# First norm of a hybrid decoder block: order of loads, two projections side by side, squares summed on GpSimd, masks moved in the program

## The chip, the cores and the metric

The kernel runs on one core of a Trainium2 chip. A core has five engines that each work through their own list of instructions in order: PE (TensorE, matmuls; PEld is its weight load), DVE (VectorE), ACT (ScalarE), POOL (GpSimd) and SP (SyncE, which here only issues DMA transfers). They wait for each other through semaphores. The metric is the device time of one execution in microseconds (us); lower is better.

## The reference

The block computes, for x of 512 tokens by 1024:

```python
h = rms_norm(x, ln1_g)                 # y = x * rsqrt(mean(x*x) + eps) * g
p = h @ w_in                           # 2464 columns
y_rwkv = rwkv7_mixer(p_rwkv, ...)      # token shift, decay, recurrence over 8 heads
y_attn = rms_norm(swa_sink_attention(q, k, v, sinks), attn_norm_g)
x = x + concatenate([y_rwkv, y_attn]) @ w_out
x = x + peer_ffn(rms_norm(x, ln2_g), ...)   # product-key choice of 128 of 16384 experts per token
return rms_norm(x, lnf_g)
```

Only the first two lines, and the constants that the mixer needs later, are touched by the change.

## The kernel before

The work runs in one line of stages: the first norm with the projections and the RWKV mixer (up to some 200 us), attention and the recurrence, the output projection with the second norm, the key products with the choice of experts, and from some 420 us to the end the experts themselves, dense matmuls over all experts for 384 tokens and gathered rows for the other 128. Each stage needs the result of the one before.

The first norm is laid out transposed: `xT` is eight tiles of 128 model columns by 512 tokens (k = 0 to 7). Per k, line 269 multiplies by ln1_g (tile `h`, DVE), `split` (lines 166 and 167) makes a high part `hhi` (a cast on ACT) and a low part `hlo` (a subtraction on DVE), and `take` squares the raw tile on ACT (lines 216 and 219) and adds the square to `n1acc` (line 220). The tiles of the squares, `n1sq`, have three buffers, so the square of k waits until the one of k - 3 has been added. The scale of the tokens, 1/rms, is applied after the projection: `scale` sums `n1acc` over the partitions with four small matmuls (`n1ss`, line 225) and takes the inverse root in twelve small DVE steps (`rsq`); `spread` brings the result to all partitions by four matmuls (`n1b`, line 232), and ACT copies it to `rb` (line 283). Every projection is multiplied by `rb` when it leaves PSUM (line 307, `pr`).

A projection (`mm3_`, lines 176 to 178) is three matmuls of 128x512 for each k: high by high, low by high, high by low. Its weights come in two halves of 256 KB, `w`, three buffers; each half is split in the same way into `wh` and `wl`, four buffers each. Projection 0 feeds the low-rank paths (`la`, then `lw` and the four `pld` products of line 330), projection 3 the first group's `k`.

On GpSimd, constants are made: identity, masks, `id32` (line 134) and the five levels of `lmask` (lines 142 to 147: for each level and quarter a memset and two affine selects), which a 32 by 32 inverse in the mixer uses from about 60 us on.

The order of instructions on each engine in this stage is not the order of the program text: a scheduler in the build sets it, engine by engine, from priorities and from its own estimates of when things are ready. Only PE's order inside the block `manual_schedule` around projection 0, `scale` and `spread` follows the text, and later projections' matmuls may still be put between. Once built, the order is fixed, and each engine takes it as it stands.

Of the kernel before, what the change touches and what calls it, by code (L numbers as in the profile page):

```python
# [7 lines left out]
F32 = mybir.dt.float32  # L8
# [9 lines left out]
S = 512  # L18
# [57 lines left out]
def _emit(ctx, tc, A, out, dbg, stop):  # L76
# [15 lines left out]
    xT = xp.tile([128, KD, S], F32, name="xT")  # L92
    vec = consts.tile([128, NVEC], F32, name="vec")
    SY.dma_start(vec, A["vec"])
    for k in range(2):
        SY.dma_start(xT[:, k, :], A["xT"][:, k, :])
    sink = consts.tile([128, 8], F32, name="sink")

    def vcol(c):
        return vec[:, c:c + 1]  # L100
# [24 lines left out]
    bones = consts.tile([128, 128], F32, name="bones")  # L125
    V.tensor_copy(bones[:, 0:64], hind[:, 0:1].to_broadcast([128, 64]))
    V.tensor_copy(bones[:, 64:128], hind[:, 1:2].to_broadcast([128, 64]))


    lmask = consts.tile([128, 5, 32], F32, name="lmask")  # L130
    id32 = consts.tile([128, 32], F32, name="id32")
    for q in range(4):
        rows = slice(32 * q, 32 * q + 32)
        GP.affine_select(out=id32[rows], in_=ones[rows, :32], pattern=[[1, 32]],
                         compare_op=OP.is_equal, fill=0.0, base=0, channel_multiplier=-1)
    for lv in range(5):
        b = 1 << lv
        n = 32 // (2 * b)
        for q in range(4):
            rows = slice(32 * q, 32 * q + 32)  # L140
            m = lmask[rows, lv, :].rearrange("p (n w) -> p n w", w=2 * b)
            GP.memset(lmask[rows, lv, :], 0.0)

            GP.affine_select(out=m[:, :, b:2 * b], in_=ones[rows, :n * b].rearrange("p (n w) -> p n w", w=b),
                             pattern=[[-2 * b, n], [0, b]], compare_op=OP.is_ge, fill=0.0,
                             base=0, channel_multiplier=1)
            GP.affine_select(out=m[:, :, b:2 * b], in_=m[:, :, b:2 * b],
                             pattern=[[2 * b, n], [0, b]], compare_op=OP.is_ge, fill=0.0,
                             base=b - 1, channel_multiplier=-1)

    c_ = consts.tile([128, 64], F32, name="c_")
    omu = c_[:, 0:14]
# [11 lines left out]
    def split(dst_hi, dst_lo, src, hi_eng=None, lo_eng=None):  # L164

        (hi_eng or SC.copy)(dst_hi, src)  # L166
        (lo_eng or V).tensor_tensor(out=dst_lo, in0=src, in1=dst_hi.bitcast(F32), op=OP.subtract)  # L167
# [40 lines left out]
    def rms(pool, n, width, name, add_eng):  # L208
# [26 lines left out]

        return take, scale, spread

    def load_w(src, name="w"):
        his, los = [], []
        for hf in range(2):  # L240
            ks = slice(4 * hf, 4 * hf + 4)
            w = wst.tile([128, 4, 128], F32, name=name, tag="w", bufs=3)
            SY.dma_start(w, src[:, ks])
            whi = wst.tile([128, 4, 128], F32R, name=name + "h", tag="wh", bufs=4)
            wlo = wst.tile([128, 4, 128], F32R, name=name + "l", tag="wl", bufs=4)
            split(whi, wlo, w)
            his += [whi[:, k] for k in range(4)]
            los += [wlo[:, k] for k in range(4)]
        return his, los

    first = {}

    def proj(i, m=128):
        whi, wlo = first.pop(i) if i in first else load_w(A["w_in"][i])
        p = pt("proj", "pj")
        yield from mm3_(p[:m], whi, wlo, hhi, hlo, m=m)
        return p[:m]


    first[0] = load_w(A["w_in"][0])  # L260
    for k in range(2, KD):
        SY.dma_start(xT[:, k, :], A["xT"][:, k, :])
    SY.dma_start(sink, A["sink"])

    take, scale, spread = rms(xp, KD, D, "n1", V)
    hhi, hlo = hl("h")
    for k in range(KD):
        h = xp.tile([128, S], F32, name="h", tag="h", bufs=3)
        V.tensor_scalar(h, xT[:, k, :], vcol(C_LN1 + k), None, op0=OP.mult)
        split(hhi[:, k, :], hlo[:, k, :], h)  # L270
        take(k, xT[:, k, :])
    with tc.manual_schedule(engines={mybir.EngineType.PE}):
        p0 = proj(0)
        while True:
            try:
                next(p0)
            except StopIteration as e:
                p0 = e.value
                break
        scale()  # L280
        pb = spread()
    rb = prep.tile([128, S], F32, name="rb", tag="rb")
    SC.copy(rb, pb)
    xst.close()

    def weave(a, na, b, nb):

        i = j = 0
        while a or b:
            if a and (not b or i * nb <= j * na):  # L290
                i += 1
                if next(a, self_) is self_:
                    a = None
            else:
                j += 1
                if next(b, self_) is self_:
                    b = None
# [22 lines left out]
    ld = [prep.tile([128, S], F32, name=f"ld{t}", tag=f"ld{t}") for t in range(NT)]  # L320

    def lora():
        yield from shifted(0, la, prep, p=p0)
        lw = prep.tile([128, S], F32, name="lw", tag="t2")
        SC.activation(lw, la, AF.Tanh)
        GP.memset(lw[64:96, :], 1.0)

        for t in range(NT):
            p = pt("chain", "pld")
            mm(p, lw[:, t * 128:(t + 1) * 128], wup, start=True, stop=True)  # L330
            SC.activation(ld[t], p, AF.Tanh, scale=0.5)
            V.tensor_scalar(ld[t], ld[t], 0.5, 0.5, op0=OP.mult, op1=OP.add)
            yield
# [11 lines left out]

    def prepare(j):
        k = prep.tile([128, S], F32, name="k", tag="k", bufs=2)
        yield from shifted(2 + 3 * j + 1, k, prep)
        kk = rwk.tile([128, S], F32, name=f"kk{j}")
        SC.activation(kk, k, AF.Identity, scale=vcol(C_KK + j))  # L350
        sq = prep.tile([128, S], F32, name="ksq", tag="t1")
        SC.activation(sq, k, AF.Square, scale=vcol(C_KK + j))
        pss = pt("chain", "kss", (128, NT, 2))
        for t in range(NT):
            mm(pss[:, t, :], sq[:, t * 128:(t + 1) * 128], hind, start=True, stop=True)
        kn = work.tile([128, NT, 2], F32, name="kn", tag="kn")
        rsqrt(kn.rearrange("p t e -> p (t e)"), pss.rearrange("p t e -> p (t e)"), 2 * NT, floor=1e-24)
        pn = pt("chain", "pn")
        for t in range(NT):
            for e in range(2):  # L360
                mm(pn[64 * e:64 * e + 64, t * 128:(t + 1) * 128], kn[:, t, e:e + 1].to_broadcast([128, 64]), ident,
                   start=True, stop=True)
        V.tensor_tensor(out=kk, in0=kk, in1=pn, op=OP.mult)
        yield
        r = prep.tile([128, S], F32, name="r", tag="r", bufs=1)
        yield from shifted(2 + 3 * j, r, prep)
        v = prep.tile([128, S], F32, name="v", tag="v", bufs=2)
        yield from shifted(2 + 3 * j + 2, v, prep)
        cs = slice(j * 128, (j + 1) * 128)

        pa = pt("chain", "pa")
        mm(pa, aup[:, cs], la, start=True, stop=True)
        B = prep.tile([128, S], F32, name="B", tag="B", bufs=2)
        SC.activation(B, pa, AF.Tanh, scale=0.5, bias=ha0[:, j:j + 1])
        kf = prep.tile([128, S], F32, name="kf", tag="t2")
        SC.activation(kf, B, AF.Identity, scale=hka[:, j:j + 1], bias=ohka[:, j:j + 1])
        V.tensor_tensor(out=k, in0=k, in1=kf, op=OP.mult)
        V.tensor_scalar(B, B, -0.5, -0.5, op0=OP.mult, op1=OP.add)
        V.tensor_tensor(out=B, in0=B, in1=kk, op=OP.mult)

        pl = pt("chain", "pl")
        for t in range(NT):
            mm(pl[:, t * 128:(t + 1) * 128], ld[t][:, cs], incl, start=True, stop=True)
        E = prep.tile([128, 8, 65], F32, name="E", tag="E", bufs=1)
        GP.memset(E[:, :, 0:1], 1.0)
        SC.activation(E[:, :, 1:65], c8(pl), AF.Exp, scale=DECAY)
        Ei = prep.tile([128, S], F32, name="Ei", tag="Ei", bufs=1)
        SC.activation(Ei, pl, AF.Exp, scale=-DECAY)
        GP.tensor_copy(DC[:, :, j:j + 1], E[:, :, 64:65])
        AR = rwk.tile([128, 8, 128], F32, name=f"AR{j}")  # L390
        V.tensor_tensor(out=AR[:, :, 0:64], in0=c8(kk), in1=E[:, :, 0:64], op=OP.mult)
        V.tensor_tensor(out=AR[:, :, 64:128], in0=c8(r), in1=E[:, :, 1:65], op=OP.mult)
        ARs.append(AR)
        V.tensor_tensor(out=B, in0=B, in1=Ei, op=OP.mult)

        V.scalar_tensor_tensor(r, r, vcol(C_RK + j), k, op0=OP.mult, op1=OP.mult)
        pbn = pt("chain", "pbn")
        mm(pbn, bones, r, start=True, stop=True)
        V.tensor_tensor(out=kk, in0=pbn, in1=v, op=OP.mult)
        BVs.append(kk)  # L400
        V.tensor_tensor(out=k, in0=k, in1=Ei, op=OP.mult)
        ops[j] = k, v, B, AR
        yield
# [1084 lines left out]
```

## Time and profile before

| | us |
|---|---|
| time, median of 3 runs | 1632.48 (1631.82 to 1632.66) |
| the profiled execution's own time | 1630.73 |
| its span, first to last instruction | 1629.0 |
| PE busy | 1572.6 (97%) |
| DVE busy | 1286.1 (79%) |
| POOL busy | 742.4 (46%) |
| ACT busy | 652.5 (40%) |

The profile is taken in one execution; all times below are counted from the start of its span. Busy time of an engine adds up its instructions; matmuls overlap, so their starts (the pitch from one to the next) say more than their lengths. A row of the timeline gives start, length, engine, line, operation, what is written and read, how many instructions are merged in it, and in brackets how long the engine sat idle before and what ended that.

### The profile page before, as it was taken

How to read it: one execution, taken by the hardware profiler on the slowest of the kernel's cores; microseconds unless marked ns; L12 is line 12 of the kernel's file. 1: busy time of each engine (PE TensorE's matmuls, PEld its weight loads, DVE VectorE, ACT ScalarE, POOL GpSimd, SP SyncE). 2: the span in 40 equal slices, each digit the busy share in tenths (PEclk: the TensorE clock that was granted, in tenths of full speed). 3: DMA queues.
4: the chain of work that ended last, by engine and by line, in shares of the span. 5: the costliest groups of instructions: out<-in, count | busy, mean ns of one | idle time of the engine just before them, and what ended most of it. 6: DMA issues, size and time to landing. Idle time of an engine off the chain costs nothing.

```text
span 1629.0 us, 30768 instructions
## 1 busy us (share of the span) xinstructions
PE 1572.6 (97%) x11869; PEld 1366.7 (84%) x11869; DVE 1286.1 (79%) x2497; ACT 652.5 (40%) x1092; POOL 742.4 (46%) x711
## 2 busy tenths in 40 slices
PE   7999999899999889999999999999999999999997
PEld 4777777797999888888988888888888888888886
DVE  6666567756899999999677788777878877887896
ACT  5333345544444344454433333333333333333334
POOL 5121123244676512222155555555655556556582
PEclk9999999999999999999999999999999999999999
DMA  4111110333232269999999888889998988989793
GB/s 143 53 42 42 59 48 2 129 124 103 79 104 91 98 214 336 348 323 354 320 345 351 304 309 320 322 299 316 331 308 301 333 312 303 321 303 339 236 311 136
DMA packets 180548, 371.18 MB, mean 228 GB/s; under 512 B 17840, under 2 KB 102320, under 8 KB 180144
## 3 DMA queue, kind: packets, MB, share of 16 engines
q1 hardware_dynamic: 137488, 226.71, 40.6%
q0 software_dynamic: 36864, 134.23, 22.9%
q10 hardware_dynamic: 6048, 8.26, 1.4%
q8 instruction: 93, 1.52, 0.4%
q14 instruction: 55, 0.45, 0.1%
HBM read 333.62 MB, written 35.52 MB: 227 GB/s over the span
## 4 chain that ended last, share of the span: by engine, by line
PE 50%; DVE 11%; DMA 3%; issue 1%; ACT 1%; POOL 1%; SPq 0%; DVEq 0%; ACTq 0%
PE acc L1359 10%; PE acc L1358 10%; PE acc L1357 10%; PE pA L178 7%; PE pA L176 7%; PE pA L177 7%; DVE O L1228 3%; DVE ul L167 2%; DVE scr L1182 2%; DVE P L1233 2%; DMA u<-in_uT_dram 2%; DMA row<-in_vB_dram,ix 1%; DMA v<-in_vB_dram 0%; PE pG L1255 0%; POOL row L1169 0%
## 5 line engine op out<-in xcount | busy, mean ns | idle before, releaser
L178 PE MATMUL pA<-h2hi,ul 128*128 128x384 f32 x1024 | 346.2, 338 | 9.9 <-DVE ul L167 5.6
L176 PE MATMUL pA<-h2hi,uh 128*128 128x384 f32 x1024 | 350.3, 342 | 1.5 <-ACT actd L969 1.5
L177 PE MATMUL pA<-h2lo,uh 128*128 128x384 f32 x1024 | 344.1, 336 | 0.0
L1169 POOL DMA_INDIRECT row<-in_u_dram,ix x128 | 175.2, 1369 | 285.7 <-DVE scr L1182 247.7
L1359 PE MATMUL acc<-vl,wh 128*128 128x512 f32 x768 | 300.3, 391 | 1.5 <-DVE vl L167 1.5
L1358 PE MATMUL acc<-vh,wl 128*128 128x512 f32 x768 | 300.0, 391 | 0.2 <-DVE wl L167 0.2
L1357 PE MATMUL acc<-vh,wh 128*128 128x512 f32 x768 | 298.9, 389 | 1.3 <-ACT vh L166 1.3
L1169 POOL DMA_INDIRECT row<-in_vB_dram,ix x128 | 196.1, 1532 | 141.1 <-DVE x L1180 115.7
L167 DVE TENSOR_TENSOR vl<-v,vh 128x1024 fp32r<-128x1024 f32 x128 | 213.9, 1672 | 35.2 <-ACT vh L166 34.4
L178 PEld LDWEIGHTS pA<-h2hi,ul 128*128 128x128 f32 x1024 | 192.8, 188 | 14.8 <-DVE ul L167 10.5
L176 PEld LDWEIGHTS pA<-h2hi,uh 128*128 128x128 f32 x1024 | 193.0, 188 | 4.7 <-ACT actd L969 1.6
L177 PEld LDWEIGHTS pA<-h2lo,uh 128*128 128x128 f32 x1024 | 193.2, 189 | 3.0
L1180 DVE SCALAR_TENSOR_TENSOR x<-row,ac,x 128x1024 f32<-128x1024 f32 x128 | 173.2, 1353 | 7.9 <-DMA row<-in_vB_dram,ix 6.0
L1359 PEld LDWEIGHTS acc<-vl,wh 128*128 128x128 f32 x768 | 144.1, 188 | 32.2 <-DVE vl L167 2.2
L1357 PEld LDWEIGHTS acc<-vh,wh 128*128 128x128 f32 x768 | 144.2, 188 | 30.0 <-ACT vh L166 1.6
L1358 PEld LDWEIGHTS acc<-vh,wl 128*128 128x128 f32 x768 | 144.1, 188 | 29.4 <-DVE wl L167 0.6
L1182 DVE SCALAR_TENSOR_TENSOR scr<-row,h2g 128x1024 f32<-128x1024 f32 x128 | 158.2, 1236 | 1.3
L166 ACT CAST uh<-u 128x1024 fp32r<-128x1024 f32 x128 | 133.9, 1046 | 62.2 <-PE pA L177 29.5
L167 DVE TENSOR_TENSOR ul<-u,uh 128x1024 fp32r<-128x1024 f32 x109 | 134.0, 1230 | 20.1 <-ACT uh L166 17.0
L166 ACT CAST vh<-v 128x1024 fp32r<-128x1024 f32 x128 | 134.0, 1048 | 0.3 <-DMA gts<-gates 0.3
L969 ACT ACTIVATE act<-pA 128x384 f32<-128x384 f32 x86 | 42.2, 491 | 131.6 <-PE pA L178 131.5
L1256 ACT ACTIVATE gst<-pG 128x512 f32<-128x512 f32 x96 | 55.8, 597 | 97.6 <-PE pG L1255 95.9
(725 smaller groups left out, 2621.0 us busy)
## 6 DMA issues: line engine op xcount, KB each, us to landing
u<-in_uT_dram SPq DMA_DIRECT2D x128, 512.0 KB, 6.4
v<-in_vB_dram SPq DMA_DIRECT2D x128, 512.0 KB, 5.9
gts<-gates SPq DMA_DIRECT2D x384, 64.0 KB, 4.5
gates<-gst SPq DMA_DIRECT2D x11, 2048.0 KB, 11.5
w<-in_w_in_dram SPq DMA_DIRECT2D x40, 256.0 KB, 2.8
wq<-in_wq_dram SPq DMA_DIRECT2D x16, 512.0 KB
acts<-actd ACTq DMA_DIRECT2D x42, 192.0 KB, 6.3
act<-acts SPq DMA_DIRECT2D x42, 192.0 KB, 7.5
```

The costliest lines, as they stand in the source:

```text
L166: (hi_eng or SC.copy)(dst_hi, src)
L167: (lo_eng or V).tensor_tensor(out=dst_lo, in0=src, in1=dst_hi.bitcast(F32), op=OP.subtract)
L176: mm(ps, whi[k][:, :m], ahi[:, k], start=k == 0, stop=False)
L177: mm(ps, whi[k][:, :m], alo[:, k], start=False, stop=False)
L178: mm(ps, wlo[k][:, :m], ahi[:, k], start=False, stop=k == KD - 1)
L1169: GP.indirect_dma_start(r_, None, A["vB"].rearrange("b p d -> (b p) d") if w_ else A["u"], bass.IndirectOffsetOnAxis(ap=ix[:, w_, jj:jj + ...
L1180: V.scalar_tensor_tensor(x2[:, 0, :], r_, ac[:, jj:jj + 1], x2[:, 0, :], op0=OP.mult, op1=OP.add)
L1182: V.scalar_tensor_tensor(scr, r_, 1.0, h2g, op0=OP.mult, op1=OP.mult, accum_out=ac[:, jj:jj + 1])
L1256: SC.activation(gst[:, :, :, t4 * 4:t4 * 4 + 4].rearrange("p n g t -> p (n g) t"), p.rearrange("p t e -> p e t"), AF.Copy, scale=1.0 / GS)
L1357: mm(o, wh[:, ts], vh[:, ds_], start=b == 0, stop=False)
L1358: mm(o, wl[:, ts], vh[:, ds_], start=False, stop=False)
L1359: mm(o, wh[:, ts], vl[:, ds_], start=False, stop=b == 127)
```

## The change

The loads come in another order: before, two tiles of `xT`, both halves of projection 0's weights, then the other six tiles of `xT`; now `xT` and halves of weights for projections 0 and 3 take turns as the table `arrive` says. The body that splits rows and weights walks the same table. Projections 0 and 3 run side by side on PE, projection 3 three steps of k behind projection 0, and `scale` and `spread` stand behind both; before, `scale` and `spread` stood behind projection 0 alone. The adds into `n1acc` go to GpSimd for k = 1 to 6 (`rms(..., GP)` in place of `V`); the last, k = 7, stays on DVE. In the program's text, the making of `lmask` and `id32` now stands behind the norm; the text of the helpers stands ahead of it, otherwise as before.

```diff
-    for k in range(2):
-        SY.dma_start(xT[:, k, :], A["xT"][:, k, :])
...
+    def load_half(src, hf, name="w"):
+        w = wst.tile([128, 4, 128], F32, name=name, tag="w", bufs=3)
+        SY.dma_start(w, src[:, 4 * hf:4 * hf + 4])
+        return w
+
+    def split_half(w, name="w"):
+        whi = wst.tile([128, 4, 128], F32R, name=name + "h", tag="wh", bufs=4)
+        wlo = wst.tile([128, 4, 128], F32R, name=name + "l", tag="wl", bufs=4)
+        split(whi, wlo, w)
+        return [whi[:, k] for k in range(4)], [wlo[:, k] for k in range(4)]
...
+    wt = {}
+    arrive = (0, (0, 0), 1, (0, 1), 2, (3, 0), 3, 4, 5, (3, 1), 6, 7)
+    for a in arrive:
+        if isinstance(a, int):
+            SY.dma_start(xT[:, a, :], A["xT"][:, a, :])
+        else:
+            wt[a] = load_half(A["w_in"][a[0]], a[1])
+    SY.dma_start(sink, A["sink"])
+
+    take, scale, spread = rms(xp, KD, D, "n1", GP)
+    hhi, hlo = hl("h")
+    early = {0: ([], []), 3: ([], [])}
+    for a in arrive:
+        if isinstance(a, int):
+            h = xp.tile([128, S], F32, name="h", tag="h", bufs=3)
+            V.tensor_scalar(h, xT[:, a, :], vcol(C_LN1 + a), None, op0=OP.mult)
+            split(hhi[:, a, :], hlo[:, a, :], h)
+            take(a, xT[:, a, :])
+        else:
+            for x, y in zip(early[a[0]], split_half(wt.pop(a))):
+                x += y
+    with tc.manual_schedule(engines={mybir.EngineType.PE}):
+        p03 = {i: pt("proj", "pj") for i in (0, 3)}
+        two = {i: mm3_(p03[i], *early[i], hhi, hlo) for i in (0, 3)}
+        for n in range(KD + 3):
+            next(two[0], None)
+            if n >= 3:
+                next(two[3], None)
+        scale()
+        pb = spread()
...
-    first[0] = load_w(A["w_in"][0])
-    for k in range(2, KD):
-        SY.dma_start(xT[:, k, :], A["xT"][:, k, :])
-    SY.dma_start(sink, A["sink"])
-
-    take, scale, spread = rms(xp, KD, D, "n1", V)
...
-        yield from shifted(0, la, prep, p=p0)
+        yield from shifted(0, la, prep, p=p03[0])
...
-        yield from shifted(2 + 3 * j + 1, k, prep)
+        yield from shifted(2 + 3 * j + 1, k, prep, p=p03[3] if j == 0 else None)
```

What the build makes of it, engine by engine, is told by the order of the instructions. The line numbers are those of each kernel; in the changed one, lines 142 and 143 are the two lines of `split`, 192 and 195 the squares, 196 the add, 201 and 208 the matmuls of `n1ss` and `n1b`, 281 to 294 the masks. In brackets stand the engines or DMA lanes whose semaphore an instruction waits for.

The first place is POOL, behind the small constants. Before, the masks follow one another:

```order
L124 MEMSET hind 64x1
L134 AFFINE_SELECT id_93<-ones 32x32
L134 AFFINE_SELECT id_93<-ones 32x32 [waits Pool_49]
L134 AFFINE_SELECT id_93<-ones 32x32
L134 AFFINE_SELECT id_93<-ones 32x32 [waits Pool_49]
L144 AFFINE_SELECT lmask<-ones 32x16 x4
```

In the changed kernel the adds of k = 1 and k = 2 stand around `id32`, and the masks of `lmask` come next:

```order
L122 MEMSET hind 64x1
L196 TENSOR_TENSOR n1acc<-n1acc,n1sq 128x512 [waits Activation_49,Pool_49]
L281 AFFINE_SELECT id_276<-ones 32x32
L281 AFFINE_SELECT id_276<-ones 32x32 [waits Pool_49]
L281 AFFINE_SELECT id_276<-ones 32x32 x2
L196 TENSOR_TENSOR n1acc<-n1acc,n1sq 128x512 [waits Activation_49,Pool_49]
L291 AFFINE_SELECT lmask<-ones 32x16
```

Two adds, each of which waits for a square of ACT, have come in ahead of the masks' main part.

The second place is POOL at the end of the masks. Before:

```order
L144 AFFINE_SELECT lmask<-ones 32x16
L147 AFFINE_SELECT lmask<-lmask 32x16
L147 AFFINE_SELECT lmask<-lmask 32x16 [waits Pool_49] x2
L502 MEMSET TF_1159 32x8x32 [waits DMAHW2_49,DMAHW5_49,DMAHW1_49,DMAHW6_49,DMAHW0_49,DMAHW7_49,DVE_49,PE_49]
L502 MEMSET TF_1159 32x8x32
```

In the changed kernel:

```order
L291 AFFINE_SELECT lmask<-ones 32x16
L294 AFFINE_SELECT lmask<-lmask 32x16
L294 AFFINE_SELECT lmask<-lmask 32x16 [waits Pool_49] x2
L196 TENSOR_TENSOR n1acc<-n1acc,n1sq 128x512 [waits Activation_49,Pool_49] x4
L513 MEMSET TF_1159 32x8x32 [waits DMAHW3_49,DMAHW1_49,DMAHW4_49,DMAHW0_49,DMAHW5_49,DVE_49,DMAHW7_49,PE_49,Pool_49]
```

The adds of k = 3, 4, 5 and 6 stand behind the last mask.

The third place is ACT, from the third square on. Before, the squares wait for adds on DVE:

```order
L219 ACTIVATE n1sq<-xT 128x512 [waits DMAHW7_49,DVE_49]
L166 CAST hhi<-h 128x512 [waits DVE_49]
L219 ACTIVATE n1sq<-xT 128x512 [waits DMAHW0_49,DVE_49]
L166 CAST hhi<-h 128x512 [waits DVE_49]
L219 ACTIVATE n1sq<-xT 128x512 [waits DMAHW1_49,DVE_49,Activation_49]
L166 CAST hhi<-h 128x512 [waits DVE_49]
L219 ACTIVATE n1sq<-xT 128x512 [waits DMAHW2_49,DVE_49,Activation_49]
```

In the changed kernel (k = 4 and 5, then `hhi` of 4 and 5, `wh` of projection 3, `hhi` of 6, the squares of k = 6 and 7, a `wh` of the next projection, and `hhi` of 7):

```order
L195 ACTIVATE n1sq<-xT 128x512 [waits DMAHW0_49,Pool_49]
L195 ACTIVATE n1sq<-xT 128x512 [waits DMAHW1_49,Pool_49]
L142 CAST hhi<-h 128x512 [waits DVE_49] x2
L142 CAST wh<-w 128x512 [waits DMAHW2_49]
L142 CAST hhi<-h 128x512 [waits DVE_49]
L195 ACTIVATE n1sq<-xT 128x512 [waits DMAHW3_49,Pool_49]
L195 ACTIVATE n1sq<-xT 128x512 [waits DMAHW4_49,Pool_49]
L142 CAST wh<-w 128x512 [waits DMAHW0_49,PE_49]
L142 CAST hhi<-h 128x512 [waits DVE_49]
```

The squares now wait for POOL, and the cast of the last row tile stands behind the squares of k = 6 and 7. On DVE, likewise, the last add into `n1acc` and one `wl` stand ahead of the last `hlo`. On PE, 40 projection matmuls stood ahead of `n1b` and 59 ahead of the first `pld`; now 48 stand ahead of `n1ss`, `n1b` follows it with nothing between, and 60 stand ahead of the first `pld`. From there on each engine's list is the same as before, but for a matmul or two that trade places with a neighbour.

## Rows read from the trace of the kernel before

**Rows 1.** The page, its part 1 (busy time of the engines) and the engines' shares of part 4 (the chain that ended last).

```profile
PE 1572.6 (97%) x11869; PEld 1366.7 (84%) x11869; DVE 1286.1 (79%) x2497; ACT 652.5 (40%) x1092; POOL 742.4 (46%) x711
...
PE 50%; DVE 11%; DMA 3%; issue 1%; ACT 1%; POOL 1%; SPq 0%; DVEq 0%; ACTq 0%
```

**Rows 2.** PE alone in three stretches of the start: stretch, length, busy us (instructions), granted clock, DMA share, GB/s.

```profile
0.00:9.15 9.15, 0.00 (x1) 1.00 0.66 216
9.15:15.20 6.05, 5.92 (x12) 1.00 0.89 331
...
21.50:31.00 9.50, 9.50 (x50) 1.00 0.42 138
```

**Rows 3.** The waits of PE over the whole span, largest first: who waited for whom, us in total, times, longest.

```profile
PE pj L176 <- ACT hhi L166: 9.5, 2, 9.1
PE pG L1255 <- DVE P L1233: 7.7, 12, 2.9
PE pA L178 <- DVE ul L167: 5.6, 7, 1.3
PE pj L176 <- DVE x2T L860: 3.8, 1, 3.8
```

**Rows 4.** The timeline of ACT.

```profile
4.12 0.63 ACT L216 ACTIVATE n1acc<-xT 128x512 f32<-128x512 f32 x1 [2.04 <-DMA xT<-in_xT_dram]
7.15 0.62 ACT L166 CAST wh<-w 128x512 fp32r<-128x512 f32 x1 [2.40 <-DMA w<-in_w_in_dram]
7.96 0.62 ACT L166 CAST wh<-w 128x512 fp32r<-128x512 f32 x1 [0.18 <-DMA w<-in_w_in_dram]
8.48 1.13 ACT L166 CAST hhi<-h 128x512 fp32r<-128x512 f32 x2
9.52 1.67 ACT L219 ACTIVATE n1sq<-xT 128x512 f32<-128x512 f32 x3
```

**Rows 5.** The timeline of DVE.

```profile
4.12 0.49 DVE L269 TENSOR_SCALAR h<-xT,vec 128x512 f32<-128x512 f32 x1 [1.08 <-DMA xT<-in_xT_dram]
...
9.22 1.28 DVE L167 TENSOR_TENSOR hlo<-h,hhi 128x512 fp32r<-128x512 f32 x2
...
10.63 0.68 DVE L220 TENSOR_TENSOR n1acc<-n1acc,n1sq 128x512 f32<-128x512 f32 x1
...
20.84 1.28 DVE L167 TENSOR_TENSOR wl<-w,wh 128x512 fp32r<-128x512 f32 x2
```

**Rows 6.** The timeline of POOL: `id32`, the start of `lmask`, its end, and what follows.

```profile
3.49 1.19 POOL L134 TENSOR_SCALAR_AFFINE_SELECT id<-ones 32x32 f32<-32x32 f32 x4
4.73 1.41 POOL L144 TENSOR_SCALAR_AFFINE_SELECT lmask<-ones 32x16 f32<-32x16 f32 x4
...
24.70 0.68 POOL L147 TENSOR_SCALAR_AFFINE_SELECT lmask<-lmask 32x16 f32<-32x16 f32 x3
25.42 2.71 POOL L502 MEMSET TF<- 32x256 f32 x8
```

**Rows 7.** Busy time in three stretches: stretch, length, then PE, PEld, DVE, ACT and POOL busy us (instructions), granted clock, DMA share, GB/s.

```profile
4.70:8.10 3.40, 0.00 (x0) 0.00 (x0) 0.81 (x2) 0.81 (x3) 2.71 (x11) 1.00 0.85 269
8.10:20.80 12.70, 10.21 (x24) 5.41 (x24) 12.60 (x25) 10.36 (x19) 10.86 (x32) 1.00 0.51 188
...
23.20:25.40 2.20, 2.20 (x11) 1.81 (x10) 1.86 (x13) 0.65 (x2) 1.73 (x10) 1.00 0.75 247
```

**Rows 8.** POOL's groups by line in the stretch 4.7 to 8.1 us: busy us, mean ns of one, idle before.

```profile
L144 POOL TENSOR_SCALAR_AFFINE_SELECT lmask<-ones 32x16 f32<-32x16 f32 x4 | 1.2, 305 | 0.2
L147 POOL TENSOR_SCALAR_AFFINE_SELECT lmask<-lmask 32x16 f32<-32x16 f32 x4 | 1.1, 286 | 0.3
L142 POOL MEMSET lmask<- 32x32 f32 x3 | 0.3, 116 | 0.2
```

**Rows 9.** The same groups in the stretch 8.1 to 20.8 us.

```profile
L144 POOL TENSOR_SCALAR_AFFINE_SELECT lmask<-ones 32x16 f32<-32x16 f32 x11 | 5.3, 483 | 0.7
L147 POOL TENSOR_SCALAR_AFFINE_SELECT lmask<-lmask 32x16 f32<-32x16 f32 x10 | 4.0, 399 | 0.6
L142 POOL MEMSET lmask<- 32x32 f32 x11 | 1.7, 157 | 0.6
```

**Rows 10.** Two-input operations of POOL elsewhere in the kernel, by tile or line: durations in ns, least, median, largest, first and last start.

```profile
L853 POOL TENSOR_TENSOR n2acc<-n2acc,n2sq x12: 732/740/1729, 323.5 to 360.8; 128x256 f32<-128x256 f32 x12
...
L1312 POOL TENSOR_TENSOR w__10340<-act,gts x1: 1005/1005/1005, 816.6 to 816.6; 128x384 f32<-128x384 f32 x1
...
L167 POOL TENSOR_TENSOR ul<-u,uh x3: 2370/2377/2392, 383.2 to 418.3; 128x1024 fp32r<-128x1024 f32 x3
```

**Rows 11.** The timeline of PE: matmuls soon after the start and later, the sums of the norm, its spread, and the first `pld`.

```profile
10.97 0.63 PE L176 MATMUL pj<-hhi,wh 128*128 128x512 f32 x1
11.40 0.63 PE L177 MATMUL pj<-hlo,wh 128*128 128x512 f32 x1
...
21.54 0.95 PE L225 MATMUL n1ss<-ones,n1acc 128*128 128x1 f32 x8
...
22.66 0.40 PE L176 MATMUL pj<-hhi,wh 128*128 128x512 f32 x1
22.89 0.40 PE L177 MATMUL pj<-hlo,wh 128*128 128x512 f32 x1
...
25.69 1.05 PE L232 MATMUL n1b<-ident,n1rs 128*128 128x128 f32 x8
...
31.07 2.94 PE L330 MATMUL pld<-wup,lw 128*128 128x512 f32 x6
```

More of the change, by code (lines that the diff above doesn't have):

```diff
@@ L127, in _emit @@
     V.tensor_copy(bones[:, 64:128], hind[:, 1:2].to_broadcast([128, 64]))
[L130 to L149, printed above, removed]
     c_ = consts.tile([128, 64], F32, name="c_")
@@ L240, in load_w @@
         for hf in range(2):
[L241 to L248, printed above, removed]
+            h_, l_ = split_half(load_half(src, hf, name), name)
+            his += h_
+            los += l_
         return his, los
-    first = {}
     def proj(i, m=128):
-        whi, wlo = first.pop(i) if i in first else load_w(A["w_in"][i])
+        whi, wlo = load_w(A["w_in"][i])
         p = pt("proj", "pj")
@@ L257, in proj @@
         return p[:m]
-    first[0] = load_w(A["w_in"][0])
-    for k in range(2, KD):
-        SY.dma_start(xT[:, k, :], A["xT"][:, k, :])
+    wt = {}
[5 more added lines that the diff above has]
+            wt[a] = load_half(A["w_in"][a[0]], a[1])
     SY.dma_start(sink, A["sink"])
-    take, scale, spread = rms(xp, KD, D, "n1", V)
+    take, scale, spread = rms(xp, KD, D, "n1", GP)
     hhi, hlo = hl("h")
[L267 to L271, printed above, removed]
-    with tc.manual_schedule(engines={mybir.EngineType.PE}):
[L273 to L279, printed above, removed]
+    early = {0: ([], []), 3: ([], [])}
[8 more added lines that the diff above has]
+                x += y
+    with tc.manual_schedule(engines={mybir.EngineType.PE}):
+        p03 = {i: pt("proj", "pj") for i in (0, 3)}
[4 more added lines that the diff above has]
+                next(two[3], None)
         scale()
@@ L284, in _emit @@
     xst.close()
+    lmask = consts.tile([128, 5, 32], F32, name="lmask")
+    id32 = consts.tile([128, 32], F32, name="id32")
+    for q in range(4):
+        rows = slice(32 * q, 32 * q + 32)
+        GP.affine_select(out=id32[rows], in_=ones[rows, :32], pattern=[[1, 32]],
+                         compare_op=OP.is_equal, fill=0.0, base=0, channel_multiplier=-1)
+    for lv in range(5):
+        b = 1 << lv
+        n = 32 // (2 * b)
+        for q in range(4):
+            rows = slice(32 * q, 32 * q + 32)
+            m = lmask[rows, lv, :].rearrange("p (n w) -> p n w", w=2 * b)
+            GP.memset(lmask[rows, lv, :], 0.0)
+            GP.affine_select(out=m[:, :, b:2 * b], in_=ones[rows, :n * b].rearrange("p (n w) -> p n w", w=b),
+                             pattern=[[-2 * b, n], [0, b]], compare_op=OP.is_ge, fill=0.0,
+                             base=0, channel_multiplier=1)
+            GP.affine_select(out=m[:, :, b:2 * b], in_=m[:, :, b:2 * b],
+                             pattern=[[2 * b, n], [0, b]], compare_op=OP.is_ge, fill=0.0,
+                             base=b - 1, channel_multiplier=-1)
     def weave(a, na, b, nb):
```

## Prediction

> **What bounds the kernel now.** I read the page first: PE is busy for 97% of the span and holds half of the chain that ended last [rows 1]. So time is won or lost where PE stands still, or where it works at its slow rate. The waits of PE come next [rows 3]: the largest is at the start, 9.1 us until the first cast of a row tile; all later ones are small, and every one of them is for something that itself hangs on the first norm. PE in stretches [rows 2] shows the rest: nothing until 9.15, then 5.92 of 6.05 us busy, and from 21.5 on no gap at all. In the first of these stretches PE is slow, too: matmuls of 512 columns start 0.43 us apart (10.97 to 11.40), later 0.23 us apart (22.66 to 22.89) [rows 11]; 512 columns in 0.43 us are 1.2 GHz, the lower of the two levels, though the column of the granted clock reads 1.00 in both stretches [rows 2].
>
> Behind that stands the chain that the change works on: the sums `n1ss` at 21.54, the spread `n1b` at 25.69, the first `pld` at 31.07 [rows 11]. POOL, off the path before, makes masks without a pause from 3.49 to 25.4 [rows 6]. That is the row that matters most, since the new order puts four adds of the norm behind the last mask.
>
> **The change part by part.** What helps: DVE loses six adds of 128x512. Two neighbours of this shape start about 0.60 us apart (two take 1.28 [rows 5]), so 3.6 us of DVE go, and PE gets a second projection to work on while rows arrive. Neither counts if the last row tile is late, and it is, by the following steps.
>
> Step 1, when the masks start. `xT` of k = 1 is now the third of the large transfers; before, the third landed at 7.15 and the fourth at 7.96 [rows 4]. Then `h` 0.5 [rows 5], its cast 0.6 and the square 0.6 (ACT starts such operations 0.52 to 0.57 us apart [rows 4]; I take 0.6 with the hand-over): the square of k = 1 is there at about 8.9. POOL, which has been through its small constants since 3.49, waits for it. The add on POOL: no row shows 128x512. The nearest are 256 columns in 0.74, 384 in 1.005 and 1024 in 2.38 us [rows 10], a line of about 2.15 ns a column, which gives 1.3 us. From both sides: above the 1.0 of 384, below the 2.4 of 1024, with the 1.73 of the slowest 256 as a warning of what a busy DVE does. I take 1.3, as DVE is waiting in the stretch that counts. So the first add ends at 10.2, the four `id32` (3.49 to 4.73, 1.2 us [rows 6]) at 11.4, the add of k = 2 (its square is ready by then) at 12.7.
>
> Step 2, when the masks end. The masks from `lmask` on took 4.73 to 25.42, that is 20.7 us for 40 selects and 16 memsets [rows 6]. They are slower while DVE is busy: a select takes 305 and 286 ns in 4.7 to 8.1, where DVE is busy for 0.81 of 3.40 us, and 483 and 399 ns in 8.1 to 20.8, where DVE has 12.60 of 12.70 [rows 7 to 9]. In the changed kernel DVE has rows to work on until about 17.3 (8 `h`, 8 `hlo` and 4 `wl`, some 10 us of work from 7.1 on) and then stands still. At the crowded rate of 21 selects and 11 memsets in 12.7 us, the stretch 12.7 to 17.3 does 7.6 selects and 4 memsets. The other 32.4 selects go at the quiet rate: 8 selects and 3 memsets in 3.40 us [rows 7, 8] are 0.37 us a select beside 0.15 a memset, 8 selects and two small memsets in the last 2.20 us [rows 7] 0.25; with 0.31, 32.4 x 0.31 + 12 x 0.15 = 11.8, and the masks end at 29.1. Bounds: 25.1 if all went at 0.25 (40 x 0.25 + 16 x 0.15 = 12.4 from 12.7), 33.4 if all took the 20.7 of before. I take 29.
>
> The Trainium skill, GPSIMD Engine Reference, section 8 "Key points", says that GpSimd shares its SBUF interfaces with VectorE and suffers from DVE instructions that read two SBUF tensors. The trace agrees, with 305 against 483 ns a select. By this rule the masks would speed up once DVE stands still, an end at 29; were the slow selects due to something else, the end would be 33.4 and the sum 4.4 us more. Its section 4.1 "Engine selection" also sends elementwise work with two inputs to VectorE, GpSimd being about half as fast; 1.3 against 0.6 us here says the same, and by that rule alone the four adds of step 3 would cost 2.8 us more on POOL than on DVE.
>
> Step 3, from the masks to the last row tile. The square of k = 6 needs the buffer that the add of k = 3 gives back, and ACT stands at it with everything behind: the square of k = 7, a `wh`, and `hhi` of k = 7, for which PE waits. That alone would free PE 4.4 us behind the masks. But DVE stands, too: its add of k = 7 needs POOL's add of k = 6, and `hlo` of k = 7 is behind it and a `wl`. So: four adds 4 x 1.3 = 5.2, DVE's add 0.6, `wl` 0.6, `hlo` 0.7: 7.1 us, at 36.1. Before, the last `hlo` was done at 20.84, where the next `wl` starts [rows 5].
>
> Step 4, the matmuls behind. PE has then 14 of the 48 matmuls to do. It has stood for over 15 us, so I price them at the pitch it showed after the idle start, 14 x 0.43 = 6.0; at the fast pitch 14 x 0.23 = 3.3. The sums start at 42.1.
>
> Step 5, sums to spread: 21.54 to 25.69 before, 4.15 us [rows 11], now with PE idle in it, since no matmul stands between. The spread starts at 46.3 instead of 25.69: 20.6 us late.
>
> Step 6, what PE has in hand. Eight more matmuls lie ahead of the spread than before (48 against 40), but ahead of the first `pld` the count is 60 against 59, and `pld` hangs on the spread by a chain of 5.4 us (25.69 to 31.07 [rows 11]) that is unchanged. So `pld` is 20.6 us late, with one matmul (0.2 us) in hand: 20.4. From there on the lists are alike, and PE was without a gap: nothing takes the delay back. The new order of DMAs costs nothing of its own: w of projection 3's second half waits for a split at about 9, and `xT` of 6 and 7 behind it on SP are there by 15, long ahead of step 3. Masks and `TF` are needed only from about 60 us.
>
> Sum: 1630.7 (the profiled execution's own time: span 1629.0 and 1.7 around it) + 20.4 = 1651.1. The median of the runs is 1.75 above that execution, so I forecast 1652.8.
>
> **The rivals.** (a) The masks don't speed up: end at 33.4, 4.4 us more than I took, 1657.2. For it: the crowded rate covers most of the trace of before; against it the quiet rates at both ends.
>
> (b) PE does not fall back to the slow pitch, or all of POOL's selects take 0.25 us: 2.7 or 3.9 us less, 1650.1 or 1648.9, both 1646.2. For it: before shows the slow pitch at the start of the program only.
>
> (c) Not slower: the adds of k = 3 to 6 reach POOL in time, as the program's text has it, with the masks behind. The place is ACT's square of k = 6, which then doesn't wait. ACT has 21 operations of 0.55 us up to `hhi` of k = 7, from 7.1 with three done: about 17.5, `hlo` at 18.8, 14 fast matmuls 3.3, the sums at 22.1, the spread at 26.2, 0.5 us later than before; with the matmul in hand 1632.8, no change. It decides if the add of k = 3 ends by about 16, when ACT comes to that square. Against it: the built order has these adds behind 40 selects, and POOL takes its list in order; the masks would have to run in 2 us.
>
> (d) The delay is taken up later, by half or more: 1643 or less. For it: PE's waits after 26 us; against it: the longest is 3.8 us [rows 3], and all of them wait for work that hangs on the norm.
>
> **How the numbers follow.** My forecast 0.62, (a) 0.14, (b) 0.15, (c) 0.04, (d) 0.05. The range: from 1645.5 (b with both, and a little of d) to 1659 (a with adds of 1.7 us, 4 x 0.4 = 1.6 more). A difference under 0.2%, 3.3 us, can't be told from no change here. Faster 0.02, same 0.04 (c), slower 0.94.
>
> **What would show it.** In the changed profile: POOL's first add at about 8.9 behind an idle time of some 5 us, the four last adds behind the masks at about 29; ACT with one idle stretch of over 10 us before a square, ended by POOL; PE with an idle stretch as long, from about 18, and a second of 3 us between `n1ss` and `n1b`; `n1b` near 46 and `pld` near 51.5; from there the rows of before, 20 us later. I am wrong if `n1b` stands before 30, if PE has no gap over 5 us after its first matmul, or if stages behind 60 us are shorter than before by more than a few us.

## The result, and the profile after

The changed kernel takes 1654.41 us (median of 4 runs, 1652.74 to 1657.54) against 1632.2 us of the kernel before (median of 4 runs): ratio 1.014, 95% interval 1.0128 to 1.0152. The profiled execution takes 1653.82 us, its span 1652.1. The forecast was 1652.8 us, in a range of 1645.5 to 1659.

POOL's timeline answers to [rows 6]; the columns are as there.

```profile
9.06 1.61 POOL L196 TENSOR_TENSOR n1acc<-n1acc,n1sq 128x512 f32<-128x512 f32 x1 [5.60 <-ACT n1sq L195]
10.62 1.63 POOL L281 TENSOR_SCALAR_AFFINE_SELECT id<-ones 32x32 f32<-32x32 f32 x4
12.33 1.60 POOL L196 TENSOR_TENSOR n1acc<-n1acc,n1sq 128x512 f32<-128x512 f32 x1
13.88 2.21 POOL L291 TENSOR_SCALAR_AFFINE_SELECT lmask<-ones 32x16 f32<-32x16 f32 x4
...
29.37 0.71 POOL L294 TENSOR_SCALAR_AFFINE_SELECT lmask<-lmask 32x16 f32<-32x16 f32 x3
30.17 5.31 POOL L196 TENSOR_TENSOR n1acc<-n1acc,n1sq 128x512 f32<-128x512 f32 x4
```

POOL idles 5.6 us for the first square, starts the masks at 13.88 where it had started them at 4.73, and comes to the four adds only at 30.17. ACT and DVE show what stood behind them, as [rows 4] and [rows 5] did before. ACT:

```profile
17.12 0.61 ACT L142 CAST hhi<-h 128x512 fp32r<-128x512 f32 x1
31.46 0.63 ACT L195 ACTIVATE n1sq<-xT 128x512 f32<-128x512 f32 x1 [13.74 <-POOL n1acc L196]
32.81 0.63 ACT L195 ACTIVATE n1sq<-xT 128x512 f32<-128x512 f32 x1 [0.71 <-POOL n1acc L196]
33.34 0.60 ACT L142 CAST wh<-w 128x512 fp32r<-128x512 f32 x1
33.85 0.61 ACT L142 CAST hhi<-h 128x512 fp32r<-128x512 f32 x1
```

DVE:

```profile
18.71 0.52 DVE L256 TENSOR_SCALAR h<-xT,vec 128x512 f32<-128x512 f32 x1
35.51 0.69 DVE L196 TENSOR_TENSOR n1acc<-n1acc,n1sq 128x512 f32<-128x512 f32 x1 [16.28 <-POOL n1acc L196]
36.12 0.68 DVE L143 TENSOR_TENSOR wl<-w,wh 128x512 fp32r<-128x512 f32 x1
36.72 0.68 DVE L143 TENSOR_TENSOR hlo<-h,hhi 128x512 fp32r<-128x512 f32 x1
```

And PE, which answers to [rows 11]:

```profile
21.86 0.40 PE L154 MATMUL pj<-hhi,wl 128*128 128x512 f32 x1
34.52 0.80 PE L152 MATMUL pj<-hhi,wh 128*128 128x512 f32 x1 [12.26 <-ACT hhi L142]
37.46 0.80 PE L153 MATMUL pj<-hlo,wh 128*128 128x512 f32 x1 [2.15 <-DVE hlo L143]
38.05 0.63 PE L154 MATMUL pj<-hhi,wl 128*128 128x512 f32 x1
38.48 0.63 PE L152 MATMUL pj<-hhi,wh 128*128 128x512 f32 x1
...
43.04 0.95 PE L201 MATMUL n1ss<-ones,n1acc 128*128 128x1 f32 x8
47.03 2.04 PE L208 MATMUL n1b<-ident,n1rs 128*128 128x128 f32 x8 [3.04 <-DVE n1rs L182]
50.47 0.79 PE L152 MATMUL pj<-hhi,wh 128*128 128x512 f32 x1 [1.40 <-DVE pr L318]
51.06 0.63 PE L153 MATMUL pj<-hlo,wh 128*128 128x512 f32 x1
...
55.76 2.96 PE L341 MATMUL pld<-wup,lw 128*128 128x512 f32 x6
```

PE stands still for 12.26 and 2.15 us ahead of the last row tile, for 3.04 between sums and spread, and for 1.40 ahead of the third projection; but for the last three ahead of the sums, the matmuls from 37.46 on and those from 50.47 up to `pld` start 0.43 us apart, the pitch of the lower level. The granted clock, which read 1.00 before [rows 2], now shows it: 0.62 for 42.1 to 56.0 us.

```profile
42.10:56.00 13.90, 9.45 (x33) 7.71 (x33) 5.40 (x17) 3.67 (x6) 3.17 (x11) 0.62 0.06 20
```

`pld` is late by 55.76 - 31.07 = 24.7 us. Later stages are moved nearly as a whole: the first sums of the second norm stand at 363.4 instead of 339.8 (23.6 late), the first of the main products at 843.7 instead of 820.1 (23.6), the last span by 23.1.

### The profile page after: what moved, and what is told of

Its sections match the earlier page's. It is cut to its first block, busy times and chain, and to the rows that moved or that the text cites. A ratio compares the mean times of both kernels' runs of the same rounds, so it can differ in the third digit from the quotient of the medians.

```text
span 1652.1 us, 30776 instructions
## 1 busy us (share of the span) xinstructions
PE 1579.2 (96%) x11869; PEld 1372.4 (83%) x11869; DVE 1286.6 (78%) x2491; ACT 653.0 (40%) x1092; POOL 744.0 (45%) x717
## 4 chain that ended last, share of the span: by engine, by line
PE 50%; DVE 11%; DMA 2%; issue 2%; ACT 1%; SPq 1%; POOL 0%; DVEq 0%; POOLq 0%; ACTq 0%
PE acc L1370 10%; PE acc L1369 10%; PE acc L1368 10%; PE pA L154 7%; PE pA L152 7%; PE pA L153 7%; DVE O L1239 3%; DVE scr L1193 2%; DVE ul L143 2%; DVE P L1244 2%; DMA gts<-gates 1%; PE pG L1266 1%; DMA row<-in_vB_dram,ix 1%; DMA acts<-actd 0%; SPq L1307 0%
```

## The experiments

Times are medians with the ratio to the kernel before and its 95% interval. All kernels compute the whole block.

**e1, the adds ahead of the masks.** GpSimd's part of the norm and the masks are held to the order of the text.

```diff
+    gst_ = ExitStack()
+    gst_.enter_context(tc.manual_schedule(engines={mybir.EngineType.Pool}))
     take, scale, spread = rms(xp, KD, D, "n1", GP)
...
                              base=b - 1, channel_multiplier=-1)
+    gst_.close()
```

> The changed kernel with GpSimd's order in the norm held to the program's text: the six adds stand ahead of every mask; all else as in the changed kernel. Theory (the four adds behind the masks are the whole loss): ACT's long wait before the square of k = 6 goes, the sums n1ss start near 25 instead of 43 us, PE has no gap over 5 us before them, and the time falls by 15 to 19 us, to 1635 to 1639; some us above the kernel before stay, since n1b still stands right behind n1ss and the next projection behind both. Rival 1 (two projections ahead of the sums are what costs): the time stays within 5 us of the changed kernel, 1649 or more. Rival 2 (the adds on GpSimd cost nothing once they are in time, the change does what its words say): 1633 or less.

Measured: 1644.86 us, 1.008 (1.0053 to 1.0107). ACT's long wait and PE's gap ahead of the last row tile are gone, and `n1ss` starts at 28.3; but the time fell by 9.5 us, not by 15 to 19. PE and DVE say why (the profiled execution took 1648.73 us, 3.9 above the median, so their waits may be somewhat long). PE:

```profile
32.33 1.47 PE L208 MATMUL n1b<-ident,n1rs 128*128 128x128 f32 x8 [3.05 <-DVE n1rs L182]
35.20 0.80 PE L152 MATMUL pj<-hhi,wh 128*128 128x512 f32 x1 [1.40 <-DVE pr L321]
...
44.03 5.49 PE L344 MATMUL pld<-wup,lw 128*128 128x512 f32 x6 [3.69 <-POOL lw L340]
```

DVE:

```profile
43.44 0.75 DVE L323 SCALAR_TENSOR_TENSOR k<-pr,vec,k 128x512 f32<-128x512 f32 x1 [6.02 <-POOL pr L320]
```

The masks, now behind the adds, run until 40.4, the memsets of `TF` follow from 40.54 to 43.24, and two small memsets that the next steps need (the first column of `pr`, at 43.30, and the rows of `lw`, at 43.46) are queued behind both. One wait for GpSimd's queue has taken the other's place. My expectation missed this, and it had the sums 3 us too early; the last section shows what held DVE there.

**e2, the adds on DVE.**

```diff
-    take, scale, spread = rms(xp, KD, D, "n1", GP)
+    take, scale, spread = rms(xp, KD, D, "n1", V)
```

> The changed kernel with the six adds back on DVE; order of loads, two projections side by side and the masks' place in the text as changed. Theory: the same as with the adds ahead of the masks, less 3.6 us of DVE time that come back ahead of the last hlo: n1ss near 25 to 26 us, 1634 to 1639 us. Rival 1 (the two projections cost): 1649 or more. Rival 2 (the new order of loads alone is a gain): under 1630.

Measured: 1638.06 us, 1.0035 (1.0022 to 1.0047), as the theory said: 16 us of the 22 are gone with the queue on GpSimd alone, and both rivals fall. `n1ss` starts at 25.2. What is left is not GpSimd's:

```profile
25.19 0.95 PE L201 MATMUL n1ss<-ones,n1acc 128*128 128x1 f32 x8
29.14 2.05 PE L208 MATMUL n1b<-ident,n1rs 128*128 128x128 f32 x8 [3.00 <-DVE n1rs L182]
32.59 0.80 PE L152 MATMUL pj<-hhi,wh 128*128 128x512 f32 x1 [1.40 <-DVE pr L318]
37.87 2.83 PE L341 MATMUL pld<-wup,lw 128*128 128x512 f32 x6
```

From spread to `pld` it takes 8.7 us as in the changed kernel, not 5.4.

**e3, seven buffers for the squares.**

```diff
-            sq = pool.tile([128, S], F32, name=name + "sq", tag="rsq", bufs=3)
+            sq = pool.tile([128, S], F32, name=name + "sq", tag="rsq", bufs=7)
```

> The changed kernel with seven buffers for the squares instead of three, so that no square waits for an add; the orders on all engines stay as they were. Theory (two blocks in series, ACT's and DVE's, and DVE's add of k = 7 ahead of the last hlo is the later one): the cast of hhi k = 7 moves from 34 to about 19 us, but the last hlo stays at 36 to 37 us, and the time stays within 2 us of the changed kernel, 1652 to 1655; PE may gain a matmul or two. Rival (ACT's wait for a buffer is what holds PE): the last hlo comes near 20 us, and the time falls by over 10 us.

Measured: 1652.89 us, 1.0123 (1.0096 to 1.0149): nothing gained that its interval can tell. ACT casts the last `hhi` at 18.10, and PE gets one matmul out of it, at 21.80; then it waits for `hlo`:

```profile
36.23 0.80 PE L153 MATMUL pj<-hlo,wh 128*128 128x512 f32 x1 [14.04 <-DVE hlo L143]
```

So of the two blocks in series, DVE's add of k = 7 ahead of the last `hlo` is the one that binds; ACT's, the longest wait by name in PE's list after the change, could go without any gain.

**e4, another PSUM bank for projection 0.**

```diff
-        p03 = {i: pt("proj", "pj") for i in (0, 3)}
+        p03 = {i: pt(("chain", "proj")[i // 3], "pj") for i in (0, 3)}
```

> The changed kernel with projection 0 in a PSUM buffer of another pair, so that the third projection need not wait until projection 0 has left PSUM; the adds stay behind the masks. Theory (the part that I had not seen: the first matmul of the third projection waited for pr on DVE, PE stood still between n1ss and n1b and again behind n1b, and worked at the slow pitch up to pld): the build now puts 12 matmuls between n1ss and n1b, so the gaps of 3.0 and 1.4 us there go and pld comes 2 to 4 us earlier with more matmuls done: 1648 to 1651. Rival (these gaps are covered, since PE has work in hand later anyway): within 1.5 us of the changed kernel.

Measured: 1649.42 us, 1.0097 (1.0068 to 1.0125), inside the expected band; its interval lies just below that of the changed kernel. With a free buffer the build puts 12 matmuls of the third projection between sums and spread:

```profile
42.19 0.95 PE L201 MATMUL n1ss<-ones,n1acc 128*128 128x1 f32 x8
...
46.18 1.13 PE L208 MATMUL n1b<-ident,n1rs 128*128 128x128 f32 x8 [0.17 <-DVE n1rs L182]
...
51.85 1.93 PE L341 MATMUL pld<-wup,lw 128*128 128x512 f32 x4
```

The spread takes 1.13 instead of 2.04 us, and `pld` follows it after 5.7 instead of 8.7 us, with 75 matmuls of projections ahead of it instead of 60. A wait of 0.97 us for `pr` is left, at 51.08. Of the 5.0 us by which the time is lower, 0.9 stand ahead of the sums already (42.19 against 43.04), which this edit doesn't touch.

**e5, the four late adds on DVE.**

```diff
-            (V if k == n - 1 else add_eng).tensor_tensor(out=acc, in0=acc, in1=sq, op=OP.add)
+            (V if k > 2 else add_eng).tensor_tensor(out=acc, in0=acc, in1=sq, op=OP.add)
```

> The changed kernel with the adds of k = 3 to 6, the four behind the masks, back on DVE; those of k = 1 and 2 stay on GpSimd. Theory (these four alone hold everything): as with all adds on DVE, 1636 to 1641 us; ACT's wait of 13.7 us goes, while POOL waits for the first two squares as in the changed kernel. Rival (any add on GpSimd costs, the first two as much as the others): over 1645.

Measured: 1639.35 us, 1.0035 (1.0023 to 1.0047), the same ratio as e2. The four adds behind the masks hold all that GpSimd cost; the two ahead of them cost nothing that shows in the time. By tile (ns least, median, largest; first and last start), in a profiled execution of 1642.23 us:

```profile
L201 PE MATMUL n1ss<-ones,n1acc x8: 166/250/251, 26.4 to 27.1; 128*128 128x1 f32 x8
...
L341 PE MATMUL pld<-wup,lw x8: 591/592/688, 38.2 to 41.5; 128*128 128x512 f32 x8
```

The sums come 4.8 us later than in the kernel before, and `pld` 7.1.

**e6, the kernel before with the adds on GpSimd.**

```diff
-    take, scale, spread = rms(xp, KD, D, "n1", V)
+    take, scale, spread = rms(xp, KD, D, "n1", GP)
```

> The kernel before with one part of the change alone: the adds of k = 1 to 6 on GpSimd; loads, projections and masks as before. In the built order all six stand at the end of the masks. Theory: POOL's masks end near 24 us, the squares of k = 4 to 7 wait for the adds, hhi of 5 to 7 behind them, n1ss comes near 35 to 37 us instead of 21.5: 1645 to 1653 us, slower by nearly as much as the whole change. Rival (the two projections or the loads make the loss): within 5 us of before.

Measured: 1643.31 us, 1.006 (1.0044 to 1.0076). The rival falls: this one edit slows the kernel before by 11 us. It is a little less than expected, since `n1ss` comes at 31.3 and not at 35 to 37; POOL, which has no idle time ahead of the masks here, ends them at about 23.7. Against my expectation, only four of the six adds stand behind the last mask; the first two are among the last masks:

```profile
19.05 1.26 POOL L220 TENSOR_TENSOR n1acc<-n1acc,n1sq 128x512 f32<-128x512 f32 x1
21.84 1.26 POOL L220 TENSOR_TENSOR n1acc<-n1acc,n1sq 128x512 f32<-128x512 f32 x1
23.69 5.97 POOL L220 TENSOR_TENSOR n1acc<-n1acc,n1sq 128x512 f32<-128x512 f32 x4
```

**e7, a version meant to beat both.** e2 and e4 together, with the sums right behind projection 0.

```diff
         for n in range(KD + 3):
             next(two[0], None)
             if n >= 3:
                 next(two[3], None)
-        scale()
+            if n == KD - 1:
+                scale()
         pb = spread()
```

> A try to beat both: adds on DVE, projection 0 in a PSUM buffer of another pair, and the sums n1ss right behind projection 0's last matmul, so that the rest of projection 3 lies under the inverse root. Theory: n1ss near 22.5, n1b near 26.5, pld near 32 us with 10 matmuls (2.3 us) more done ahead of it than before: 1628 to 1633 us, within 2 us of the kernel before or a little better. Rival (the last hlo is later by the extra splits of projection 3's weights, and this is not paid back): 1634 to 1637.

Measured: 1630.6 us, 0.9988 (0.9978 to 0.9997), as the theory said, and 24 us under the changed kernel. By tile:

```profile
L201 PE MATMUL n1ss<-ones,n1acc x8: 164/250/250, 23.2 to 23.9; 128*128 128x1 f32 x8
...
L208 PE MATMUL n1b<-ident,n1rs x8: 275/275/347, 26.7 to 27.6; 128*128 128x128 f32 x8
...
L342 PE MATMUL pld<-wup,lw x8: 592/592/697, 32.2 to 35.6; 128*128 128x512 f32 x8
```

`pld` is 1.1 us later than before, with 71 matmuls of projections done ahead of it instead of 59. The gain, 0.12%, is below the 0.2% that I called tellable, though its interval leaves 1 out.

**e8, the kernel before with the new order of loads alone.**

```diff
-    for k in range(2):
-        SY.dma_start(xT[:, k, :], A["xT"][:, k, :])
...
-    first[0] = load_w(A["w_in"][0])
-    for k in range(2, KD):
-        SY.dma_start(xT[:, k, :], A["xT"][:, k, :])
+    arrive = (0, (0, 0), 1, (0, 1), 2, 3, 4, 5, 6, 7)
+    for a in arrive:
+        if isinstance(a, int):
+            SY.dma_start(xT[:, a, :], A["xT"][:, a, :])
+        else:
+            wt[a] = load_half(A["w_in"][a[0]], a[1])
...
```

> The kernel before with the order of loads alone changed: tiles of xT and the two halves of projection 0's weights take turns, and are split in that order; one projection ahead of the sums, adds on DVE. Theory: PE's first matmul comes at 5.8 instead of 9.15 us and its slow pitch ends earlier, but DVE, busy without a gap from 7.8 to 21 us, sets the last hlo; it starts some of its work up to 1 us earlier: 0 to 2 us faster than before, 1630 to 1632.5. Rival (PE's start is what counts): 3 us faster, under 1629.

Measured: 1631.15 us, 0.9989 (0.9979 to 0.9998). PE starts at 6.12 instead of 9.15, but `n1ss` comes at 20.7 instead of 21.5, and that 0.8 us is about what the time shows. If any part of the change does a little good, it is the loads; but this gain, 0.11%, too, is below the 0.2% that I called tellable.

**e9, what held e1.**

```diff
-        GP.memset(pr[:m, 0:1], 0.0)
+        V.memset(pr[:m, 0:1], 0.0)
...
-        GP.memset(lw[64:96, :], 1.0)
+        V.memset(lw[64:96, :], 1.0)
```

> The kernel of e1 (six adds ahead of every mask on GpSimd), with the two small memsets behind the masks, the first column of pr and the rows of lw, moved from GpSimd to DVE. In e1 the first pld waited 3.7 us for POOL's memset of lw, and DVE 6.0 us for POOL's memset of pr, both queued behind the masks. Theory (these two waits are what kept e1 above the version with the adds on DVE): the first pld comes near 40 instead of 44 us, and the time falls by 3 to 6 us, to 1638.5 to 1642. Rival (it is DVE, held up beside the adds on POOL, that kept e1 above): within 1.5 us of e1, 1643.4 to 1646.4.

Measured: 1640.91 us, 1.0058 (1.0044 to 1.0071), with the first `pld` at 41.2 instead of 44.0. The two medians are 4.0 us apart, as the theory said; but the interval of the ratio overlaps e1's (1.0053 to 1.0107), so the size is less certain than the place, which the traces show. The rest above e2 fits `n1ss`, 28.2 here and 25.2 there.

## Why the prediction was right, and where it was off

The mechanism was right: four adds behind the masks, ACT and DVE behind the adds, PE behind DVE. By its steps:

- Step 1 had the masks start at 12.7; they did at 13.88. The square was there at 9.06 (8.9 forecast), but an add beside a busy DVE took 1.6 instead of 1.3, and the `id32` 1.63 instead of 1.2.
- Step 2 had them end at 29; they ended at 30.1. DVE had rows to work on until 19.2, not 17.3, and the masks did speed up once it stood still: a select took 504 and 476 ns before 19 us, and 216 and 210 ns behind, even less than the 0.31 that I priced. That GpSimd shares its SBUF interfaces with VectorE is what the Trainium skill, GPSIMD Engine Reference, section 8 "Key points", says; these rows agree. Rival (a), masks that stay slow, falls, and so does the half of (b) by which all selects take 0.25.
- Step 3 forecast 7.1 us from the masks to the last `hlo`; from 30.17 to its end at 37.40 there are 7.2. That DVE and not ACT binds was said there, and e3 shows it.
- Step 4 forecast 14 matmuls 0.43 us apart: from 37.46 to the sums at 43.04 there are 5.6 us, and only the last three are fast. The other half of (b) falls.
- Step 5 forecast 4.15 us from sums to spread; 43.04 to 47.03 is 3.99.
- Step 6 was off. It called the chain from spread to `pld` "unchanged", 5.4 us; it took 8.7. I had the 12 matmuls there follow the spread at once, and priced neither them nor the spread at the slow pitch. In fact the spread took 2.04 us instead of 1.05. Two projections ahead of the sums hold both PSUM buffers of that pair, so the third waits until `pr` has read the first (the 1.40 us <- DVE pr), and then runs at the slow pitch, 5.3 us for the 12: 2.04 + 1.40 + 5.3 = 8.7. `lw`, which `pld` reads, was complete at 53.27, so 2.5 us of this are PE's own backlog. `pld` was 24.7 late, not 20.4: 0.7 from the steps ahead, 3.3 from here, and the matmul in hand, 0.2, gave nothing. e4 shows this term: with the other bank `pld` follows the spread 3.1 us sooner.
- "Nothing takes the delay back" was nearly right: of 24.7 us at `pld` 23.1 are left at the end. The 1.6 go in small steps: the first use of `lmask` is 24.2 us late (84.3 against 60.1), the second norm 23.6. Rival (d) falls.
- The median came within 1.6 us of the forecast partly by luck. The profiled execution's own time was forecast at 1651.1 and was 1653.82, 2.7 more; but the median stands 0.6 above that execution here, and I had added 1.75.

Rival (c), the adds in time, is not what the changed kernel did. e5 puts the same four adds in time on DVE and gives 1639.35, not the 1632.8 that (c) stated. Two terms of (c) were too small. It had the sums at 22.1; they came at 26.4 in e5, where DVE has the four adds to do, and at 28.3 in e1, where GpSimd does them. (Its own count was off by half a microsecond the other way: 18 operations of 0.55 us from 7.1 on end at 17.0, not 17.5.) And from spread to `pld` it took 7.9 us, not 5.4: the term of step 6 was missing there, too. So the loss of 22 us has two parts: some 15 us from the four adds' place in GpSimd's queue (the changed kernel against e5), and some 7 us, all that is left in e5. At `pld` these 7 are 4.8 from the later sums, which stand behind 48 matmuls instead of 26, and the rest behind them. e7 takes away all of it but 1.1 us at `pld`, with an earlier place for the sums, the other bank and all adds on DVE; what each of these does in e7 was not taken apart.

## What to carry to other kernels

An engine takes its list as the build made it, whatever the text says; before work is given to an idle engine, read where the list puts it, and what stands behind it on that engine and behind its consumers on theirs. When a wait is removed, look at once for what is queued behind the work that was pushed back, as e1's small memsets were. Of a matmul that may be hoisted under a chain, ask first whether its PSUM buffer is free.

## What the runs showed of the hardware that I had not expected

DVE was held up by GpSimd's adds, and not only the other way. The eight `h`, one SBUF input and a scalar, took 472 to 486 ns with the adds on DVE; in e1 half of them were far longer, those that ran beside the adds on POOL (8.3 to 11.3 and 13.8 to 18.3 us). First e2, then e1:

```profile
L256 DVE TENSOR_SCALAR h<-xT,vec x8: 472/478/486, 4.1 to 19.3; 128x512 f32<-128x512 f32 x8
```

```profile
L258 DVE TENSOR_SCALAR h<-xT,vec x8: 474/949/1502, 4.1 to 22.0; 128x512 f32<-128x512 f32 x8
```

An add on POOL, which took 1.33 to 1.63 us in e1, can thus cost DVE 1 us as well, so the 3.6 us that I credited DVE with were partly taken back.

The low level came back after a pause of 3 us in one kernel and not in another. The spread stands behind a pause of 3.04 us in the changed kernel, of 3.00 in e2 and of 3.04 in e3; in this order:

```profile
L208 PE MATMUL n1b<-ident,n1rs x8: 421/421/551, 47.0 to 48.7; 128*128 128x128 f32 x8
```

```profile
L208 PE MATMUL n1b<-ident,n1rs x8: 421/421/554, 29.1 to 30.8; 128*128 128x128 f32 x8
```

```profile
L208 PE MATMUL n1b<-ident,n1rs x8: 275/275/347, 45.2 to 46.0; 128*128 128x128 f32 x8
```

The granted clock of these stretches reads 0.50, 0.50 and 1.00. How long PE had been at the fast pitch ahead of the sums does not sort them: since 42.3 in the changed kernel (sums at 43.04), since 17.4 in e2 (25.19), since 39.8 in e3 (41.17). What decides it stays open.
